# Feed-forward products of a hybrid attention block: the stationary operand read as every other number of 1 KB

## The chip, the cores and the metric

The kernel runs on one core of one Trainium2 chip. The metric is the device time of one execution in microseconds (us); the time of a kernel is the median of its runs. Matmuls run on TensorE (PE in the profile, its weight loads PEld), elementwise work on VectorE (DVE), ScalarE (ACT) and GpSimd (POOL); SyncE (SP) issues transfers.

## The reference, cut to what matters

One block of a network for 512 tokens of width 1024: attention over selected keys, a recurrent branch, gates, a first layer norm, a feed-forward part of width 4096, a gated addition and a second layer norm. The change concerns the feed-forward part:

```
D_MODEL = 1024
SEQ = 512
D_FF = 4 * D_MODEL
...
        h = layer_norm(DEEPNORM_ALPHA * h + merged @ w_out[l], ln1_g[l], ln1_b[l])
        ff = jnp.square(jax.nn.relu(h @ w_ff1[l])) @ w_ff2[l]
        r = DEEPNORM_ALPHA * h + ff
        r = r + jax.nn.sigmoid(r @ w_ple_gate[l]) * (p[l] @ w_ple_proj[l])
        h = layer_norm(r, ln2_g[l], ln2_b[l])
```

All inputs and outputs are float32.

## The kernel before, in words

Every large product is made from operands that are split in two numbers of the type float32r, a high part and a low rest, and three matmuls take the place of one: high by high, high by low, low by high. ACT makes the high part (a cast), DVE or POOL the rest (a subtraction).

The first feed-forward product, `h @ w_ff1`, lies in `ff1` (the matmul is at L969). Its columns are done in four groups of 1024. In each group the product is seen as one of matrices of 2 by 2 blocks and made with seven block products, `P1` to `P7`, in place of eight; sums of blocks go in, and `ff1_sums` puts the results together. So there are 28 steps. In a step the stationary operand is 128 columns of a block of the weights (`w1h`, `w1l`, made by `w1_factor`), four such pieces `b`; the moving operand is 256 tokens of a block of the transposed h (`hcH`, `hcL`, made by `h_factors` with `split` at L114 and L120). For each of the four pieces there are three kinds of product of four matmuls each over the 512 rows of the block: 48 matmuls a step, 1344 in all, and before each of them its stationary operand is loaded. A matmul writes 128 by 256 numbers.

The second product, `relu(...)^2 @ w_ff2`, lies in `ff2` (the matmul is at L1200), again as seven block products for each of four blocks of rows: 28 steps. Here the stationary operand is 128 tokens of the activations (`ah`, `al`), two such pieces `s`, and the moving operand 512 columns of the weights (`wh`, `wl`): 24 matmuls a step, 672 in all, each with a load of its own. A matmul writes 128 by 512 numbers.

`issue_after` chains the matmuls of both products in the order in which they are written; ACT's and DVE's work for them goes in the order of `queued`. The operands of a step are made while the step before it runs, in pairs of buffers. Weights come by transfers into `w1q` and `b`; some blocks get a second block added by a transfer that accumulates, which POOL issues (L896 and L1050). The two kinds of step take turns only at one place: the first of `ff2`'s steps is issued before the last of `ff1`'s.

In the built program every operand of both products begins 32 bytes past a multiple of 64 bytes. Counted in 256 bytes, the stationary operand that is loaded next begins 64 bytes after the place where the moving operand begins in `ff1`, and at the same place in most of `ff2`.

Of the kernel before, what the change touches and what calls it, by code (L numbers as in the profile page):

```python
# [7 lines left out]
F32 = mybir.dt.float32  # L8
# [6 lines left out]
P = 128  # L15
S = 512
D = 1024
# [6 lines left out]
DFF = 4096  # L24
# [30 lines left out]
    return ap.bitcast(F32)  # L55


@with_exitstack
def block_kernel(ctx: ExitStack, tc: tile.TileContext, t, out):
    nc = tc.nc  # L60
    te, ve, se, ge, sy = nc.tensor, nc.vector, nc.scalar, nc.gpsimd, nc.sync
# [8 lines left out]
    def open_pool(name, side=None, space=None, reuse="tile"):  # L70
        kw = {}
        if side:
            kw["side"] = side
        if space:
            kw["space"] = space
        cm = tc.tile_pool(name=name, bufs=1, reuse_waits=reuse, **kw)
        p = cm.__enter__()
        return p, (lambda: cm.__exit__(None, None, None))
# [9 lines left out]

    def misc(name):
        return ps_pool.tile([P, 512], F32, tag="misc", bufs=4, name=name)  # L90

    const, close_const = open_pool("const", side="left")
# [4 lines left out]
    rawpool, close_raw = open_pool("raw", side="right")  # L99
# [13 lines left out]
    def split(src, hi, lo, lo_eng=None, copy=None):  # L113
        (copy or se.copy)(hi, src)  # L114
        low(lo_eng or ve, lo, src, hi)

    def low(eng, lo, src, hi):

        if eng is not ge:
            return eng.tensor_sub(lo, src, f(hi))  # L120
        w = src.shape[-1]
        for j in range(src.shape[1]):
            for c in range(0, w, 256):
                o = slice(c, min(c + 256, w))
                eng.tensor_sub(lo[:, j][..., o], src[:, j][..., o], f(hi[:, j][..., o]))
# [30 lines left out]
    def transpose4(dst, src, k0):  # L156
        for k in range(4):
            t_ = te.transpose(dst[:, k * P:(k + 1) * P], src[:, (k0 + k) * P:(k0 + k + 1) * P], ident)
        return t_
# [6 lines left out]
    for _ in range(20):  # L166
# [7 lines left out]
    ge.affine_select(out=bias0, in_=bias0, compare_op=OP.is_ge, fill=MASKED, base=0,  # L174
                     pattern=[[-1, P]], channel_multiplier=1)
    mhalf = const.tile([P, 16], F32, name="mhalf")
    ve.memset(mhalf, -0.5)


# [47 lines left out]
    for k in range(KD):  # L227
        wh, wl = (w[:, k % 2] for w in kvw[k // 2][1:])
        for kind in range(3):
            for i in range(NT):  # L230
                te.matmul(b1[i][:, :208], (xH, xL, xH)[kind][:, k, i * P:(i + 1) * P], (wh, wh, wl)[kind],
                          start=k == 0 and kind == 0, stop=k == KD - 1 and kind == 2)
# [20 lines left out]
    def stacks(src, n, name, tag, bufs):  # L253

        st = att.tile([P, n, P], F32R, tag=tag, bufs=bufs, name=name)
        for g in range(n // 4):
            ps = misc(name + "p")
            transpose4(ps, src.rearrange("p n a b -> p (n a b)"), g * 4)
            v = ps.rearrange("p (h q) -> p h q", h=4)
            o = st[:, g * 4:g * 4 + 4, :]  # L260
            se.copy(o, v)
            ve.tensor_sub(o[64:128], v[64:128], f(o[64:128]))
        return st
# [58 lines left out]
    for i in range(NT):  # L322
        ve.tensor_scalar(wi[:, i, :], b1[i][:, 192:200], IDX_W, None, op0=OP.mult)
        ps = misc("kp")
        for n, o in enumerate((128, 0)):
            k2 = att.tile([P, 1, 2, 64], F32, tag="k2", bufs=2, name="k2")
            rope(b1[i][:, o:o + 64], i, 1, k2, ve)
            te.transpose(ps[:, n * P:(n + 1) * P], k2.rearrange("p n a b -> p (n a b)"), ident)
        split(ps[:, 0:P], kiH[:, i * P:(i + 1) * P], kiL[:, i * P:(i + 1) * P])
        split(ps[:, P:2 * P], kaH[:, i * P:(i + 1) * P], kaL[:, i * P:(i + 1) * P])  # L330
        split(b1[i][:, 64:128], vHL[:, i, 0:64], vHL[:, i, 64:128])
        se.copy(vH0[:, i, 0:64], b1[i][:, 64:128])
# [9 lines left out]
    for i in range(1, NT):  # L342
        n = (i + 1) * P
        q2 = q2s[i % 2]
        rope(b3[i], i, HEADS, q2, ve)
        st = stacks(q2, HEADS, "qi", "qs", 2)
        sc = att.tile([P, n], F32, name=f"sc{i}")
        for h in range(HEADS):
            ps = misc("lg")
            te.matmul(ps[:, :n], st[:, h, :], kiH[:, :n], start=True, stop=False)  # L350
            te.matmul(ps[:, :n], st[:, h, :], kiL[:, :n], start=False, stop=True)
            rl = att.tile([P, S], F32, tag="rl", bufs=2, name="rl")[:, :n]
            se.activation(rl, ps[:, :n], AF.Relu)
            if h == 0:
                ve.tensor_scalar(sc, rl, wi[:, i, h:h + 1], None, op0=OP.mult)
            else:
                ve.scalar_tensor_tensor(sc, rl, wi[:, i, h:h + 1], sc, op0=OP.mult, op1=OP.add)
        ge.affine_select(out=sc[:, i * P:], in_=sc[:, i * P:], compare_op=OP.is_ge, fill=NEG_CAUSAL, base=0,
                         pattern=[[-1, P]], channel_multiplier=1)
        scores[i] = sc  # L360
# [356 lines left out]
    hcH, hcL = {}, {}  # L717
# [57 lines left out]
    def h_factors(i):  # L775

        o = slice(i % 2 * P, i % 2 * P + P)

        def put(n, ps):
            split(ps.rearrange("p (k q) -> p k q", k=4), hcH[n][:, :, o], hcL[n][:, :, o])  # L780

        ps = [misc("hps0"), misc("hps1")]
        for kk in range(2):
            turned[:] = [transpose4(ps[kk], r[:, i, :], kk * 4)]
        if i < 2:
            for kk in range(2):
                se.copy(hb[kk][:, :, o], ps[kk].rearrange("p (k q) -> p k q", k=4))
                put((A11, A12)[kk], ps[kk])
            return
        a22 = ln.tile([P, 512], F32, tag="a22", bufs=1, name="a22")  # L790
        se.copy(a22, ps[1])
        put(A22, ps[1])
        v = [p_.rearrange("p (k q) -> p k q", k=4) for p_ in ps]
        ve.tensor_sub(ps[1], ps[0], a22)
        p2, p3 = misc("hps2"), misc("hps3")
        v2, v3 = (p_.rearrange("p (k q) -> p k q", k=4) for p_ in (p2, p3))
        ve.tensor_sub(v2, v[1], hb[0][:, :, o])
        ve.tensor_add(v3, v2, hb[1][:, :, o])
        put(S4, p3)
        put(S1, ps[1])  # L800
        ve.tensor_sub(v[0], hb[0][:, :, o], v[0])
        put(S3, ps[0])
        put(S2, p2)
# [146 lines left out]
    def w1_banks(t, n):  # L950
        e = t % 2 * 3
        return sets[{P1: e, P6: e, P2: 3 - e if t else 1, P5: 1}.get(n, 2)]
# [3 lines left out]
    def ff1(t, n, ws):  # L956

        hi, lo = ws
        ah, al = hcH[HALF[n]], hcL[HALF[n]]
        for kinds in (((hi, ah), (hi, al)), ((lo, ah),)):  # L960
            for b in range(4):
                ps = w1_banks(t, n)[b // 2][:, b % 2 * 256:b % 2 * 256 + 256]

                def product():
                    for w, a in kinds:
                        for k in range(4):

                            fresh = n not in (P6, P4) and w is hi and a is ah and k == 0 and b % 2 == 0
                            mm = te.matmul(ps, w[:, k, b * P:(b + 1) * P], a[:, k], start=fresh, stop=w is lo and k == 3,  # L969
                                           skip_group_check=True)  # L970
                    mms.append(mm)

                if mms:
                    with tc.issue_after(mms[-1].ins):
                        product()
                else:
                    product()
# [203 lines left out]
    banks, before = {}, []  # L1181
# [9 lines left out]
    def ff2(d, n, e, ops):  # L1191

        (wh, wl), (ah, al) = ops
        fresh = e == 0 and (d == 0 if n in (P1, P6) else n in (P5, P2, P4, P7))
        for s, kind in ((0, 0), (0, 1), (1, 0), (1, 1), (0, 2), (1, 2)):
            tok = slice(s * P, (s + 1) * P)

            def product():
                for q in range(4):
                    mm = te.matmul(banks[n, s], (al if kind == 1 else ah)[:, q, tok], (wl if kind == 2 else wh)[:, q],  # L1200
                                   start=fresh and kind == 0 and q == 0, stop=kind == 2 and q == 3, skip_group_check=True)
                before.append(mm)

            if before:
                with tc.issue_after(before[-1].ins):
                    product()
            else:
                product()
# [79 lines left out]
    for k, (d, n, e) in enumerate(steps):  # L1288
# [32 lines left out]
        if (d, n, e) in GATE_STEPS:  # L1321
            load_gate(0, GATE_STEPS.index((d, n, e)))
        ff2(d, n, e, ops)
        if (d, n) == (1, P4):
            gate_inputs(e)
# [82 lines left out]
```

## Time and profile before

| | |
|---|---|
| runs | 770.44, 774.37 and 776.04 us, median 774.37 us |
| the profiled execution | 776.13 us, of which 774.4 us from the first instruction to the last |
| PE busy in it | 760.9 us (98%), 4332 matmuls and 4332 loads |
| the other engines | DVE 596.9 us (77%), ACT 419.4 us (54%), POOL 268.7 us (35%) |
| matmuls of `ff1` (L969) | 407.5 us to 569.6 us |
| matmuls of `ff2` (L1200) | 560.1 us to 720 us |

A matmul is shown longer than the distance to the next one, because matmuls are pipelined: how fast they go is read from the distance between two starts, or from the time that a row of many took together, and not from the mean of one. The chain of work that ended last is followed back from the last instruction; 20% of the span on it is L969 and 20% L1200.

### The profile page before, as it was taken

The page shows a single profiled execution, that of the slowest core. Times are in us where ns is not written, and L with a number is a line of the kernel's source. Part 1 is how long each engine was busy: PE and PEld are TensorE (multiplying, and loading weights), DVE is VectorE, ACT ScalarE, POOL GpSimd, SP SyncE. Part 2 cuts the span into 40 slices and gives each one's busy share as a digit, 9 for nine tenths or more (in the row PEclk, how much of TensorE's full clock was granted, in tenths as well). Part 3 has the DMA queues.
Part 4 walks back from the last instruction along what each step waited for, and adds up shares of the span by engine and source line. Part 5 has one row for each costly group of instructions (what it writes and reads, how often), then busy time and mean ns, then how long its engine had stood idle before and what let it go on. Part 6 is the DMA issues. An engine that isn't in the chain of part 4 may idle for free.

```text
span 774.4 us, 11502 instructions
## 1 busy us (share of the span) xinstructions
PE 760.9 (98%) x4332; PEld 664.3 (86%) x4332; DVE 596.9 (77%) x988; ACT 419.4 (54%) x637; POOL 268.7 (35%) x332
## 2 busy tenths in 40 slices
PE   9899999999999999999999999999999999999995
PEld 8678888888988888878889999999988888888885
DVE  6669999966547987477796757576788988998558
ACT  5346556698756543443266575656565555656221
POOL 7627464434346445670142120303010101116341
PEclk9999999999999999999999999999999999999999
DMA  7424232232232202348069996947597799895302
GB/s 236 136 55 129 64 81 56 82 96 56 55 83 81 69 15 68 96 142 327 22 213 196 330 255 191 236 103 113 112 222 195 135 390 315 145 185 181 102 27 109
DMA packets 78072, 110.43 MB, mean 143 GB/s; under 512 B 3776, under 2 KB 39104, under 8 KB 76736
## 3 DMA queue, kind: packets, MB, share of 16 engines
q1 hardware_dynamic: 59664, 72.78, 28.5%
q0 software_dynamic: 13920, 27.27, 20.5%
q10 hardware_dynamic: 4432, 9.65, 3.6%
q8 instruction: 34, 0.56, 0.3%
q14 instruction: 22, 0.18, 0.1%
HBM read 101.29 MB, written 8.39 MB: 142 GB/s over the span
## 4 chain that ended last, share of the span: by engine, by line
PE 87%; DVE 7%; POOL 2%; DMA 2%; issue 1%; ACT 1%; SPq 0%; DVEq 0%; POOLq 0%; ACTq 0%
PE pf L969 20%; PE pf L1200 20%; PE pg L152 4%; PE pg L154 4%; PE pg L153 4%; PE po L152 2%; PE po L153 2%; PE po L154 2%; PE pu L152 1%; PE pu L154 1%; PE pu L153 1%; PE ptp L460 1%; POOL wul L145 1%; PE mqc L152 1%; PE mo L152 1%; PE mv L153 1%
## 5 line engine op out<-in xcount | busy, mean ns | idle before, releaser
L823 DVE TENSOR_TENSOR w1l<-w1q,w1h 128x1024 fp32r<-128x1024 f32 x55 | 64.9, 1222 | 35.6 <-ACT w1h L823 35.0
L823 DVE TENSOR_TENSOR wl<-b,wh 128x2048 fp32r<-128x2048 f32 x28 | 64.7, 2312 | 10.7 <-ACT wh L823 10.7
L823 ACT CAST w1h<-w1q 128x1024 fp32r<-128x1024 f32 x55 | 55.2, 1048 | 24.4 <-PE pf L969 19.8
L896 POOL DMA_DIRECT2D w1q<-in_w_ff x24 | 29.2, 1254 | 111.9 <-DVE w1l L823 108.0
L145 POOL TENSOR_TENSOR wgl<-wgr,wgh 128x256 fp32r<-128x256 f32 x64 | 50.3, 819 | 44.8 <-ACT wgh L142 40.4
L1050 POOL DMA_DIRECT2D b<-in_w_ff x14 | 17.9, 1279 | 133.2 <-DVE wl L823 133.2
L1200 PE MATMUL pf<-wh,ah 128*128 128x512 f32 x216 | 58.1, 391 | 0.0
L1200 PE MATMUL pf<-wh,al 128*128 128x512 f32 x216 | 57.8, 389 | 0.0
L823 ACT CAST wh<-b 128x2048 fp32r<-128x2048 f32 x28 | 53.5, 1909 | 3.5 <-DMA b<-in_w_ff 3.5
L1200 PE MATMUL pf<-wl,ah 128*128 128x512 f32 x216 | 53.5, 390 | 0.0
L154 PE MATMUL pg<-xH,wgl 128*128 128x512 f32 x128 | 50.5, 395 | 0.0
L153 PE MATMUL pg<-xL,wgh 128*128 128x512 f32 x128 | 50.3, 393 | 0.0
L152 PE MATMUL pg<-xH,wgh 128*128 128x512 f32 x128 | 50.1, 391 | 0.0
L1200 PEld LDWEIGHTS pf<-wh,al 128*128 128x128 f32 x216 | 40.6, 188 | 8.5
L1200 PEld LDWEIGHTS pf<-wh,ah 128*128 128x128 f32 x216 | 40.3, 188 | 8.7 <-ACT wh L823 0.4
L1200 PEld LDWEIGHTS pf<-wl,ah 128*128 128x128 f32 x216 | 40.5, 188 | 8.4
L145 POOL TENSOR_TENSOR wul<-wur,wuh 128x128 fp32r<-128x128 f32 x64 | 35.3, 584 | 21.5 <-ACT wuh L142 17.7
L823 DVE TENSOR_TENSOR c<-c,pf 128x512 f32<-128x512 f32 x48 | 30.5, 682 | 10.2 <-ACT c L823 10.2
L823 ACT ACTIVATE c<-c 128x1024 f32<-128x1024 f32 x12 | 12.7, 1060 | 31.3 <-DVE c L823 31.3
L744 POOL TENSOR_TENSOR lag<-lag,mhalf 128x1 f32<-128x1 f32 x8 | 7.6, 950 | 62.9 <-DVE lag L743 62.9
L153 PEld LDWEIGHTS pg<-xL,wgh 128*128 128x128 f32 x128 | 24.0, 188 | 4.5
L152 PEld LDWEIGHTS pg<-xH,wgh 128*128 128x128 f32 x128 | 24.1, 188 | 4.5
(396 smaller groups left out, 2309.1 us busy)
## 6 DMA issues: line engine op xcount, KB each, us to landing
b<-in_w_ff POOLq DMA_DIRECT2D x14, 1024.0 KB, 9.0
w1q<-in_w_ff POOLq DMA_DIRECT2D x24, 512.0 KB, 7.5
w1q<-in_w_ff SPq DMA_DIRECT2D x9, 1024.0 KB, 5.7
wgr<-in_w_in SPq DMA_DIRECT2D x16, 512.0 KB, 3.8
b<-in_w_ff SPq DMA_DIRECT2D x8, 1024.0 KB, 8.2
wor<-in_w_out SPq DMA_DIRECT2D x8, 512.0 KB, 3.9
b<-in_w_ff ACTq DMA_DIRECT2D x4, 1024.0 KB, 6.0
wpgr<-in_w_ple_gate SPq DMA_DIRECT2D x8, 512.0 KB, 8.9
```

The costliest lines, as they stand in the source:

```text
L145: (lo_eng or ge).tensor_sub(lo[:, k:k + n], raw[:, k:k + n], f(hi[:, k:k + n]))
L152: te.matmul(ps, sh, mh, start=first, stop=False, **kw)
L153: te.matmul(ps, sh, ml, start=False, stop=False, **kw)
L154: return te.matmul(ps, sl, mh, start=False, stop=last, **kw)
L460: te.transpose(ps[:, slot * P:(slot + 1) * P], prs[slot // 2][:, slot % 2, j * P:(j + 1) * P], ident)
L744: ge.tensor_tensor(out=ag[:, 3:4], in0=ag[:, 2:3], in1=mhalf[:, 0:1], op=OP.pow))
L823: order_of[engine] = getattr(engine, op)(*args, **kw)
L896: ge.dma_start(out=tl[:, k], in_=w1_rows(t, W1_ADD[n])[:, k], accum_op=OP.add)
L969: mm = te.matmul(ps, w[:, k, b * P:(b + 1) * P], a[:, k], start=fresh, stop=w is lo and k == 3, skip_group_check=True)
L1050: return ge.dma_start(out=tl, in_=rows_of(g, w), accum_op=OP.add)
L1200: mm = te.matmul(banks[n, s], (al if kind == 1 else ah)[:, q, tok], (wl if kind == 2 else wh)[:, q], start=fresh and kind == 0 and q == 0, ...
```

## The change

A helper `alternate` gives every other number of a row: of 256 numbers (1 KB) the even ones are the block 0, the odd ones the block 1. The stationary operands of both products are read so: 128 numbers, 8 bytes apart, over 1 KB, where they were 128 numbers in a row, over 512 bytes.

For `ff1` the columns of `w_ff1` are put in that order in the input's memory ahead of the launch, so that the pieces `b` 0 and 1, and 2 and 3, alternate. For `ff2` the tokens alternate: `h_factors` writes the 128 tokens of a block to every other place of `hcH` and `hcL`, so the activations come out in the same order, and `ff2` reads its pieces `s` 0 and 1 from even and odd places. The moving operands are read in a row as before, and the results of `ff2` have the tokens of one block in a row again.

Two unused tiles, of 32 and of 224 bytes, move what lies behind them in the two halves of the on-chip memory: in the built program all operands of the two products begin at multiples of 64 bytes (the odd block 4 bytes further), and the distance in 256 bytes between stationary and moving operand is what it was. DVE fills the two tiles once at the start. Besides these two fills every engine has the same instructions in the same order.

```
+def alternate(ap, which):
+
+    return ap.rearrange("p k (j s) -> p k s j", s=2)[:, :, which]
...
     mhalf = const.tile([P, 16], F32, name="mhalf")
+    ve.memset(const.tile([P, 8], F32, name="pad"), 0.0)
+    ve.memset(rawpool.tile([P, 56], F32, name="rawpad"), 0.0)
     ve.memset(mhalf, -0.5)
...
         def put(n, ps):
-            split(ps.rearrange("p (k q) -> p k q", k=4), hcH[n][:, :, o], hcL[n][:, :, o])
+            split(ps.rearrange("p (k q) -> p k q", k=4), alternate(hcH[n], i % 2), alternate(hcL[n], i % 2))
...
-                            mm = te.matmul(ps, w[:, k, b * P:(b + 1) * P], a[:, k], start=fresh, stop=w is lo and k == 3,
+                            mm = te.matmul(ps, alternate(w[:, :, b // 2 * 256:b // 2 * 256 + 256], b % 2)[:, k], a[:, k], start=fresh, stop=w is lo and k == 3,
                                            skip_group_check=True)
...
         for s, kind in ((0, 0), (0, 1), (1, 0), (1, 1), (0, 2), (1, 2)):
-            tok = slice(s * P, (s + 1) * P)
+            at = alternate(al if kind == 1 else ah, s)
...
-                    mm = te.matmul(banks[n, s], (al if kind == 1 else ah)[:, q, tok], (wl if kind == 2 else wh)[:, q],
+                    mm = te.matmul(banks[n, s], at[:, q], (wl if kind == 2 else wh)[:, q],
                                    start=fresh and kind == 0 and q == 0, stop=kind == 2 and q == 3, skip_group_check=True)
...
+    arrays["in_w_ff1"] = np.ascontiguousarray(arrays["in_w_ff1"].reshape(1, D, DFF // 256, 2, P)
+                                              .transpose(0, 1, 2, 4, 3).reshape(1, D, DFF))
```

## Rows read from the trace of the kernel before

**Rows 1.** The page: busy time of each engine.

```profile
PE 760.9 (98%) x4332; PEld 664.3 (86%) x4332; DVE 596.9 (77%) x988; ACT 419.4 (54%) x637; POOL 268.7 (35%) x332
```

**Rows 2.** The chain that ended last: start us, us, what (the feed-forward part).

```profile
407.63 152.64 PE pf L969 x1296
...
563.99 5.66 PE pf L969 x48
569.65 138.18 PE pf L1200 x608
```

**Rows 3.** Busy time by stretch: stretch, its us, engines, clock, DMA share, GB/s.

```profile
407.40:560.00 152.60, 152.60 (x1297) 152.56 (x1297) 106.77 (x116) 93.21 (x111) 27.82 (x23) 1.00 0.80 193
...
569.60:720.00 150.40, 150.40 (x670) 124.12 (x669) 134.87 (x106) 82.53 (x63) 33.17 (x29) 1.00 0.86 223
```

**Rows 4.** Timeline of PE: another product with moving operands of 256 columns.

```profile
182.39 0.28 PE L152 MATMUL mv<-mvwh,xH 128*128 128x256 f32 x1
...
184.98 0.28 PE L153 MATMUL mv<-mvwl,xH 128*128 128x256 f32 x1
...
185.65 0.28 PE L152 MATMUL mv<-mvwh,xH 128*128 128x256 f32 x1
...
186.67 0.28 PE L152 MATMUL mv<-mvwh,xH 128*128 128x256 f32 x1
```

**Rows 5.** Timeline of PE: two rows of matmuls with moving operands of 512 columns.

```profile
59.70 0.40 PE L153 MATMUL aq<-aqwl,xH 128*128 128x512 f32 x1
...
60.86 0.39 PE L152 MATMUL aq<-aqwh,xH 128*128 128x512 f32 x1
...
97.81 0.39 PE L154 MATMUL pg<-xH,wgl 128*128 128x512 f32 x1
...
99.17 0.39 PE L154 MATMUL pg<-xH,wgl 128*128 128x512 f32 x1
```

**Rows 6.** The chain: eight transposes, moving operands of 128 columns.

```profile
380.78 0.87 PE hps L158 x8
```

**Rows 7.** Timeline of PE and its stretch at half the clock: 512 columns.

```profile
28.87 0.63 PE L154 MATMUL iq<-iqwh,xL 128*128 128x512 f32 x1
...
30.15 0.63 PE L154 MATMUL iq<-iqwh,xL 128*128 128x512 f32 x1
...
27.40:30.70 3.30, 3.30 (x10) 2.51 (x9) 1.99 (x11) 3.05 (x10) 1.86 (x2) 0.50 0.01 2
```

**Rows 8.** Who waited for whom, 560 to 725 us: us in total, times, longest.

```profile
ACT ah L823 <- PE pf L1200: 53.8, 23, 2.6
...
ACT wh L823 <- DMA b<-in_w_ff: 3.5, 2, 2.3
...
PEld pf L1200 <- ACT wh L823: 0.4, 1, 0.4
```

**Rows 9.** Who waited for whom, 400 to 560 us.

```profile
ACT w1h L823 <- PE pf L969: 19.8, 10, 2.7
```

**Rows 10.** Groups by form, 375 to 425 us: the writes of `hcH` and `hcL`, one each.

```profile
L114 ACT CAST hc0H<-hps 128x512 fp32r<-128x512 f32 x2 | 1.2, 599 | 0.0
L120 DVE TENSOR_TENSOR hc0L<-hps,hc0H 128x512 fp32r<-128x512 f32 x2 | 1.4, 677 | 1.4 <-ACT hc0H L114 1.4
```

**Rows 11.** Timeline of DVE and PE at the start.

```profile
1.16 0.07 DVE L177 MEMSET mhalf<- 128x16 f32 x1
...
1.26 4.63 PE L167 MATMUL idle<-warm 128*128 128x256 f32 x20 [1.26 <-DVE mhalf L177]
```

## The prediction

> **What bounds the kernel now.** I read the page first: PE is busy for 98% of the span, no other engine for more than 77% [rows 1]. Then the chain of waits: through the feed-forward part it is PE alone, matmul after matmul, with no wait of another engine in between [rows 2]. [...] So whatever one matmul of these two products gains or loses goes to the end of the span, 1344 and 672 times, as long as ACT, DVE and the transfers keep up.
>
> How far apart do the matmuls stand? In the first product 1296 of them take 152.64 us, 117.8 ns each, and the last 48 take 5.66 us, 117.9 ns each; in the second 608 take 138.18 us, 227.3 ns each [rows 2]. How much of that could go is read from other products of the same shapes in this trace. With 256 moving columns the distance has two values, each held for a whole row of matmuls: from 182.39 to 184.98 us there are 22 distances, 117.7 ns each, and from 185.65 to 186.67 us nine, 113.3 ns each, in the same product with the same kind of operands [rows 4]. With 512 columns the usual value is (99.17 - 97.81)/6 = 226.7 ns; the five distances from 59.70 us have 232 ns [rows 5]. And 113.3 is half of 226.7: this looks like the pace of the moving operand alone, with 4.4 ns of something else on top in most products of 256 columns.
>
> What the something is, rows only hint at. The load by itself is short enough: transposes with 128 moving columns, where the load is the longer part, stand 0.87/8 = 109 ns apart [rows 6], below 113. Load and moving operand read the same memory at the same time, and their relative place is fixed by the addresses and the start of the row; that two levels hold over whole rows of equal instructions [rows 4] speaks for readers that do or don't get in each other's way. The first product sits at the upper level throughout.
>
> **The change part by part.** *The load of the first product.* In the time of one matmul the moving operand goes through 1 KB. The load went through 512 bytes and now goes through 1 KB: the two readers go at the same pace, a fixed distance apart, where before one passed over the other. If the 4.4 ns come from their meeting, a fixed distance of 64 bytes takes them away: 1344 x (117.8 - 113.3) = -6.0 us. This is the value that I take, since the lower level is the nearest row with the same shape, and no row of 256 columns at full clock goes below it. The bounds are far on both sides: 109 ns (the load alone, [rows 6]) would be -11.8 us; 4.4 ns twice over 113.3 ns, because the load now touches twice as much memory, would be 122.2 ns, +5.9 us.
>
> [...]
>
> *The load of the second product.* It has 227 ns to hide in, and the distance is within 0.6 ns of the lower level already: 672 x (227.3 - 226.7) = -0.4 us if all of it goes. I take -0.3 us. [...] On the other side the 232 ns of rows 5 would be +3.2 us.
>
> *Other operands at multiples of 64 bytes.* The some 1400 matmuls of 512 columns outside the feed-forward part keep their shapes and steps; most are at the lower level of rows 5. I take 0; bounds -1.2 us and +1.2 us (a sixth of them changes between the 232 and the 226.7 ns of rows 5).
>
> *The writes of `hcH` and `hcL` at every other place.* There are 14 casts on ACT of about 0.6 us and 14 subtractions on DVE of about 0.68 us [rows 10], same sizes as before. I take their length as unchanged. If each took half as long again, ACT would have 4.2 us and DVE 4.8 us more, spread from 381 to 414 us; PE has the projections of the second input to do meanwhile, and at the end of this stretch only a microsecond or two of it could show, +1 us at most.
>
> *The two fills on DVE.* They stand ahead of the fill `mhalf`, for whose end the twenty warm-up matmuls wait [rows 11]. Two of about 0.07 us delay these by 0.15 us; the first real matmuls wait for their inputs afterwards, so I count 0.1 us.
>
> *What is late next.* If PE gets faster by 4% in the first product, its step of 48 matmuls shrinks from 5.65 to 5.44 us. ACT waits for PE there 10 times, 19.8 us in all [rows 9], and DVE is busy 107 of 152.6 us [rows 3]: both follow. In the second product DVE is busy 134.87 of 150.4 us [rows 3], 90%, and ACT waited for PE 23 times [rows 8]; one load of weights came just too late, 0.4 us of PE [rows 8]. With a second product as it was, this stays.
>
> The sum: -6.0 - 0.3 + 0.1 = -6.2 us. The profiled execution took 776.13 us, its span 774.4 us; the difference is set up around it and stays. The median of the runs, 774.37 us, lies 1.8 us below the profiled execution, so I take the sum from the median: 768.2 us.
>
> **The rivals.**
>
> *More is freed than the lower level.* If the moving operand's own pace of 226.7 ns were also the work of loads, both products could fall to what rows 6 and 7 bound: the first to 109 ns (-11.8 us), the second to 213 ns (-9.4 us), in all 753 us; DVE would then have 134.87 us of work in 141 us and would begin to delay steps, so 755 us is nearer. [...]
>
> *The change doesn't do what it says.* The 4.4 ns may have nothing to do with where the load reads: the first product stays at 117.8 ns, 774 us. For: rows 4 switch levels with the same operands in the same order, so the start of a row matters, not only addresses. [...]
>
> *The two readers meet more often.* A load that touches 1 KB has twice the chances to get in the way of the moving operand, and where they go at the same pace at the same place, as in the second product, they may do so all along. Then the first product goes to 122.2 ns (+5.9 us) and the second to the 232 ns of rows 5 (+3.2 us): 783.5 us. It decides from the point where the first product's distance is above 118 ns. For: the 232 ns of rows 5 show that with 512 columns, too, a matmul can be held up. Worse still, a load of twice the length, 218 ns, would set the distance of the first product: 1344 x 100 ns, +134 us, 908 us. Nothing in the trace excludes it, since none of its loads has a step.
>
> **How the numbers follow.** The forecast, 766 to 770 us, has 0.4; more freed (752 to 762 us) 0.17; no effect (773 to 776 us) 0.2; more meetings (778 to 788 us) 0.2; the long load 0.03. The range 754 to 784 us leaves out half of the first and third rival's ends and the long load. A measurement of this kernel tells about 1%, 7.7 us, from no change. Faster by over that, below 766.6 us: the first rival and the lower part of the forecast, where the other products gain too, 0.3. Slower by over 1%, above 782.1 us: most of the third rival and the long load, 0.2. The rest, 0.5, is within 1%.
>
> **What would show it.** In the changed kernel's chain the 1296 matmuls of the first product should take 147 us in place of 152.64, and 608 of the second 137.8 us. [...] The loads shown should stay as long as they are. The prediction is wrong above all if loads with a step take longer than loads in a row, which this trace can't show, or if the levels are set by the start of a row and not by the addresses.

## The result, and the profile after

| | runs | median | lowest to highest |
|---|---|---|---|
| before | 4 | 772.64 us | 770.44 to 776.04 us |
| after | 4 | 784.14 us | 783.21 to 784.93 us |

The ratio on record is 1.0133, with a 95% interval of 1.0093 to 1.0172 (the two medians by themselves give 1.0149): the change makes the kernel slower by 10 to 11.5 us, where 6 us less had been forecast. Every run of after lies above every run of before. The profiled execution of after took 784.38 us, its span 782.7 us, against 776.13 and 774.4 us before: 8.3 us more.

The page first, busy time of each engine in the kernel after:

```profile
PE 768.2 (98%) x4332; PEld 671.0 (86%) x4332; DVE 597.9 (76%) x990; ACT 420.0 (54%) x637; POOL 267.8 (34%) x332
```

The same 4332 matmuls have 7.3 us more of PE, and PE is still busy for 98% of the span. DVE has two instructions more, the fills, and 1 us more work. So the lost time is to be looked for in the distances of matmuls. The chain of the kernel after (start us, us, what), to be laid beside [rows 2]:

```profile
407.93 155.52 PE pf L977 x1296
563.45 3.69 PE pf L1208 x16
567.14 5.76 PE pf L977 x48
572.90 24.26 PE pf L1208 x104
...
665.27 50.66 PE pf L1208 x216
```

In the first product 1296 matmuls take 155.52 us, 120.0 ns each, where they took 117.8 ns; the last 48 take 5.76 us, 120.0 ns as well. In the second, 104 take 24.26 us, 233.3 ns each, where it was 227.3 ns. Those 227.3 ns hold the 0.4 us that PE lost behind a late load of weights [rows 8]; without it they are (138.18 - 0.4)/608 = 226.6 ns, the usual value of [rows 5]. The starts of the pieces add up to the whole: the first product begins 0.3 us later than in [rows 2], the second 3.25 us later, and its 608 matmuls end at 665.27 + 50.66 = 715.93 us, 8.1 us later than before (569.65 + 138.18 = 707.83). So the first product has cost 2.95 us and the second 715.93 - 572.90 - 138.18 = 4.85 us.

Was PE held up by others? The stretches of the two products in after (stretch, its us, then busy us and instructions of PE, PEld, DVE, ACT and POOL, granted clock, DMA share, GB/s):

```profile
407.70:563.30 155.60, 155.60 (x1298) 155.56 (x1298) 107.22 (x117) 93.81 (x112) 27.82 (x23) 1.00 0.79 190
572.90:728.00 155.10, 154.17 (x667) 127.36 (x667) 135.08 (x106) 82.00 (x63) 33.37 (x29) 1.00 0.85 217
```

Granted clock and work of the other engines are nearly those of [rows 3]. PE has no idle time in the first stretch and 155.10 - 154.17 = 0.93 us in the second. That is one late load. Timeline of ACT and of PE in after at that place (in brackets the idle time before, and who ended it):

```profile
663.31 1.91 ACT L831 CAST wh<-b 128x2048 fp32r<-128x2048 f32 x1 [3.44 <-DMA b<-in_w_ff]
```
```profile
665.27 1.20 PE L1208 MATMUL pf<-wh,ah 128*128 128x512 f32 x4 [0.93 <-ACT wh L831]
```

A transfer into `b` landed late, ACT's cast of it waited 3.44 us, and PE lost 0.93 us behind the cast. So of the 8.1 us, 0.3 lie ahead of the feed-forward part, 2.95 in the first product and 608 x (233.3 - 226.7) = 4.0 in the distances of the second; the 0.8 us left are what late loads cost more in this execution than in that of before.

The loads themselves, a group of the second product from 570 to 720 us, in after:

```profile
L1208 PEld LDWEIGHTS pf<-wh,ah 128*128 128x128 f32 x208 | 40.0, 193 | 9.6 <-ACT wh L831 1.4
```

The mean load is shown with 193 ns, and 64 loads of the first product with 194 ns in the middle. In the kernel before both groups have 188 ns. Both grew by 5 to 6 ns.

### The profile page after: what moved, and what is told of

It reads as the page before. It is cut to its first block, busy times and chain, and to the rows that moved or that the text cites. A ratio compares the mean times of both kernels' runs of the same rounds, so it can differ in the third digit from the quotient of the medians.

```text
span 782.7 us, 11504 instructions
## 1 busy us (share of the span) xinstructions
PE 768.2 (98%) x4332; PEld 671.0 (86%) x4332; DVE 597.9 (76%) x990; ACT 420.0 (54%) x637; POOL 267.8 (34%) x332
## 4 chain that ended last, share of the span: by engine, by line
PE 80%; DVE 10%; DMA 5%; issue 4%; ACT 1%; SPq 0%; POOL 0%; DVEq 0%; POOLq 0%; ACTq 0%
PE pf L977 21%; PE pf L1208 11%; PE pg L158 4%; PE pg L160 4%; PE pg L159 4%; DMA b<-in_w_ff 3%; PE pu L160 2%; PE po L160 2%; PE po L159 2%; PE po L158 2%; PE pu L158 2%; PE pu L159 2%; PE ptp L468 1%; PE mqc L158 1%; PE mo L158 1%
## 5 line engine op out<-in xcount | busy, mean ns | idle before, releaser
L831 ACT CAST ah<-uH 128x1024 fp32r<-128x1024 f32 x12 | 12.6, 1052 | 29.2 <-PE pf L1208 29.2
```

The source lines that it names most:

```text
L831: order_of[engine] = getattr(engine, op)(*args, **kw)
```

## The experiments

The theory after this result: **the step makes the load longer**, and in the first product the load (120.0 ns) now outlasts the moving operand (113.3 ns) and sets the distance. The rivals: the new beginnings of the operands do it, not the step; or the step makes load and moving operand get in each other's way, as the third rival of the prediction says. One question came with it: where do the 4.4 ns between 113.3 and 117.8 ns come from, if no step takes them away?

**The step alone** (`e1_step_alone`): the two tiles go, so the operands begin 32 bytes past a multiple of 64 bytes, as before.

```
-    ve.memset(const.tile([P, 8], F32, name="pad"), 0.0)
-    ve.memset(rawpool.tile([P, 56], F32, name="rawpad"), 0.0)
```

> The step of two numbers alone, without the two unused tiles: all operands again 32 bytes past a multiple of 64. Theory A (the step costs, the alignment does nothing): first product 120.0 ns a matmul, second 233.3 ns, as with the whole change, 782 us. Theory B (the alignment costs, the step is harmless or good): first product at 117.8 ns or 113.3 ns, second at 226.7 ns, 768 to 774 us.

Measured: 782.87 us median of 4 runs (782.65 to 783.31), 1.0148 times the kernel before (1.0093 to 1.0203). The chain of this kernel:

```profile
408.00 155.52 PE pf L975 x1296
572.97 141.84 PE pf L1206 x608
```

The same 120.0 and 233.3 ns, as theory A has it, and no late load this time. Its span, 781.6 us, is 7.2 us above that of before: 155.52 - 152.64 = 2.9 us in the first product and 141.84 - 138.18 = 3.7 us in the second make up 6.6 of it. So the loss belongs to the step, and beginnings at multiples of 64 bytes are not needed for it.

**Steps of 1, 2, 4 and 1 in the four groups** of the first product (`e2_steps_by_group`), the rest as after:

```
+STEP = (1, 2, 4, 1)
...
+    def piece(t, w, b):
+        s = STEP[t]
+        o = b // s * s * P
+        return alternate(w[:, :, o:o + s * P], b % s, s)
...
+                            mm = te.matmul(ps, piece(t, w, b)[:, k], a[:, k], start=fresh, stop=w is lo and k == 3,
```

> All operands at multiples of 64. The four groups of the first product read their stationary operand with steps of 1, 2, 4 and 1 numbers (the input's columns are put in the order that fits); the second product as in the change. Theory A1 (what counts is how much memory the load goes through: 512 bytes, 1 KB, 2 KB): 117.8, 120.0, about 124 to 127, 117.8 ns. [...] Theory A3 (load and moving operand meet when they go at the same pace; at another pace they don't stay together): step 4 no worse than 118 to 120 ns. Theory B (alignment): the groups with step 1 are at 120 ns too.

Measured: 818.22 us, one run. The chain of this kernel, one piece from each group:

```profile
408.95 35.13 PE pf L985 x310
...
446.97 38.04 PE pf L985 x317
...
486.91 77.26 PE pf L985 x328
...
566.96 30.15 PE pf L985 x266
```

113.3, 120.0, 235.5 and again 113.3 ns. The distance goes with the step, group by group in one execution. A1's 124 to 127 ns and A3's 118 to 120 ns don't fit the 235.5 ns at a step of 4. Why a step of 2 costs 6.7 ns was not shown. And the groups in a row stand at 113.3 ns here, without any step: the lower level that the prediction wanted is there when nothing but the tiles has changed, or by chance. That is taken up below.

**The same with half the moving operand** (`e3_steps_half`). Each matmul of the first product takes 128 of its 256 tokens; half of the product is left out. Then the load should be the longer of the two at every step (109 ns in a row, from [rows 6], against half of 113.3 ns for the moving operand, an estimate), and the distance shows it by itself: if the step makes the load longer, 120.0 ns stay at a step of 2; if the two get in each other's way, steps of 1 and 2 are alike.

```
-                            mm = te.matmul(ps, piece(t, w, b)[:, k], a[:, k], start=...
+                            mm = te.matmul(ps[:, k % 2 * P:k % 2 * P + P], piece(t, w, b)[:, k],
+                                           a[:, k, k % 2 * P:k % 2 * P + P], start=...
```

> As the kernel with the steps by group, but each matmul of the first product takes only 128 of its 256 tokens (even k the first half, odd k the second), so half of the first product's work is left out and the load is the longer part: the distance is the load's own time. [...] Theory A3 (two readers in each other's way, the load by itself as long as ever): 109 ns with step 1 and 2 alike, or nearly.

Measured: 846.73 us. Pieces of this kernel's chain with steps of 1, 2 and 4:

```profile
409.00 35.06 PE pf L985 x314
...
445.91 38.16 PE pf L985 x318
...
485.86 76.36 PE pf L985 x327
```

111.7, 120.0 and 233.5 ns. With half of the moving operand the distances at steps 2 and 4 are what they were with all of it. So 120.0 ns is the load's own length, and not a meeting with the moving operand, which has only half the time to meet in. (A load in a row, 111.7 ns, is a little longer than the 109 ns that the prediction read from transposes.) The third stretch must be read with care, since the clock fell in it (columns as above):

```profile
446.00:484.00 38.00, 38.00 (x319) 38.00 (x319) 26.61 (x29) 21.97 (x27) 7.25 (x6) 1.00 0.86 228
485.50:488.30 2.80, 2.80 (x14) 2.80 (x13) 1.87 (x2) 1.84 (x2) 0.28 (x1) 1.00 1.12 202
488.50:562.00 73.50, 73.50 (x316) 73.50 (x317) 26.44 (x29) 25.39 (x29) 6.77 (x6) 0.50 0.38 87
```

The comparison of steps 1 and 2 lies at a granted clock of 1.00. That of step 4 lies at 0.50, but for its beginning. Timeline of PE there:

```profile
485.22 1.10 PE L985 MATMUL pf<-hc0H,w1h 128*128 128x128 f32 x4
...
488.03 0.91 PE L985 MATMUL pf<-hc0L,w1h 128*128 128x128 f32 x3
```

Twelve distances in 2.81 us at a granted clock of 1.00 are 234 ns each, so step 4 takes the same at both levels, and nearly the 235.5 ns of the run above.

**Four distances, with the step** (`e4_distance_scan`). In the first product the stationary operand begins 192, 0, 64 and 128 bytes, counted in 256 bytes, after the moving operand, one distance for each group; in the second 128 bytes.

```
+        hi, lo = (pools[1].tile([P, 2112], F32R, tag="w1" + x, ...)[:, 16 * t:16 * t + 2048]
+                  .rearrange("p (a b) -> p a b", a=4) for x in "hl")
...
+                gap.append(late.tile([P, 32], F32, name="gap"))
```

> Steps of 2 and multiples of 64 as in the change, but the stationary operand begins 192, 0, 64 and 128 bytes (in 256) after the moving one in the four groups of the first product, and 128 in place of 0 bytes in the second. [...] Theory A3 (at the same pace the distance decides whether they meet): distances differ by 4 ns or more, some at 113.3 ns; the second product moves away from 233.3 ns, towards 226.7 ns.

Measured: 783.41 us. A piece each from the first, second and fourth group, and one of the second product:

```profile
408.93 38.08 PE pf L978 x313
...
448.95 39.12 PE pf L978 x326
...
529.95 33.06 PE pf L978 x273
...
573.59 24.08 PE pf L1214 x104
```

121.7, 120.0 and 121.1 ns (the third group has 120.0 ns too); 231.5 ns in the second product. No distance goes below 120 ns, so the prediction's "fixed distance" has nothing to work on: the load comes first. The place of the two operands adds 1.7 ns at most in the first product, and 128 bytes take 1.8 ns off the 233.3 ns of the second.

**The two tiles alone** (`e5_tiles_alone`), with loads in a row: before, and the two fills.

> The two unused tiles alone: all operands at multiples of 64 bytes, every load again 128 numbers in a row. Theory D (the alignment takes 4.4 ns from the first product, the step costs more than that in both): first product 113.4 ns, second 226.7 ns, 6 us less than before, 764 to 768 us. Rival (the two groups at 113.4 ns in the run with steps by group owe it to what lies beside them): 117.8 ns and no difference.

Measured: 769.89 us median of 12 runs against 775.12 us of 17, ratio 0.9945 (0.9919 to 0.9971). Its chain:

```profile
408.52 146.88 PE pf L971 x1296
564.57 137.88 PE pf L1202 x608
```

113.3 ns: the whole forecast gain of the first product, without the step. It looked as if beginnings at multiples of 64 bytes were the cause. Two scans asked whether beginning or distance counts: loads in a row, distances of 64, 96, 128 and 192 bytes in the four groups, the moving operand at a multiple of 64 bytes (`e6_row_scan_at_64`) or 32 bytes past one (`e7_row_scan_at_32`).

```
+        hi, lo = (pools[1].tile([P, 2112], F32R, ...)[:, (0, 8, 16, 32)[t]:(0, 8, 16, 32)[t] + 2048]
```

> As the kernel with the two tiles alone, but in the four groups of the first product the stationary operand begins 64, 96, 128 and 192 bytes (in 256) after the moving one: in the second group it is 32 bytes past a multiple of 64 while the moving operand is at one. Theory D1 (the load's own alignment counts): 113.4, 117.8, 113.4, 113.4 ns. Theory D2 (the moving operand's alignment counts): 113.4 ns in all. Theory D3 (the distance counts): differences between 64, 128 and 192.

> The kernel before, but with the same four distances: the moving operand 32 bytes past a multiple of 64 throughout, the stationary one at a multiple of 64 in the second group alone. Theory D1 (the load's own alignment): 117.8, 113.4, 117.8, 117.8 ns. Theory D2 (the moving operand's): 117.8 ns in all. Theory D3 (the distance): differences between 64, 128 and 192 bytes.

Measured: 775.87 and 774.08 us. Two pieces of the first one's chain:

```profile
408.93 36.15 PE pf L972 x319
...
446.94 38.64 PE pf L972 x322
```

From such pieces of all groups, in ns:

| distance | 64 | 96 | 128 | 192 bytes |
|---|---|---|---|---|
| at a multiple of 64 | 113.3 | 120.0 | 118.7 | 117.8 |
| 32 past one | 117.8 | 117.3 | 118.7 | 117.8 |

So a matmul with a load in a row can be held up too, by an amount that changes with the distance inside one unbroken row of matmuls, up to the 120.0 ns of a load with a step. Beginnings alone don't explain it: at 64 the first line of the table falls to 113.3 and at 192 it doesn't. Each line is one execution, so what it shares with the level of that execution can't be told apart: at 64 bytes the two lines show just the two levels.

**Is it the beginning, or the execution?** The kernel of the two tiles was run again in 12 runs (`e13_tiles_again`), and beside it one in which two small unrelated tiles, `invf` and `wi`, are moved to another pool, while beginnings and distances stay (`e14_tiles_and_moved`).

```
-    invf = const.tile([P, 32], F32, name="invf")
+    invf = att.tile([P, 32], F32, name="invf")
...
-    wi = const.tile([P, NT, HEADS], F32, name="wi")
+    wi = att.tile([P, NT, HEADS], F32, name="wi")
```

> The two unused tiles alone, a second time and with more executions: are loads in a row at multiples of 64 bytes what puts the first product on the lower of its two levels (113.3 and 117.8 ns, 6 us apart in all)? Theory H (the alignment does it): most executions near 769 us, as in the first run of this kernel, while the kernel before is spread over both levels. Theory I (the moment at which a row of matmuls starts decides, whatever the alignment): about the same share of both levels in both kernels.

> The two unused tiles, and two small tiles of the attention part in another pool, so that everything in the left half lies 256 bytes lower: the same alignment and the same distances in both products as with the two tiles alone; this is the first product of the four runs with two kinds of loads in the second, three of which stood at 117.8 ns and one at 113.3 ns. Theory H (alignment): most executions near 769 us. Theory I (the start of the row): both levels, a good part of them near 775 us.

Measured: 771.95 us median against 773.64 us of 23 runs of before, ratio 1.0004 (0.997 to 1.0038); and 770.0 us, ratio 0.9989 (0.9955 to 1.0023). The chain of the first, the same program as the one with 146.88 us above:

```profile
407.82 152.64 PE pf L971 x1296
```

117.8 ns. So one program stood at 113.3 ns in one execution (770.69 us) and at 117.8 ns in another (776.60 us): the addresses alone don't set the level. The difference of 5.9 us is that of the row, 1344 x 4.43 ns = 6.0 us. `e14_tiles_and_moved` stood at 113.3 ns (146.88 us for 1296, 771.22 us in all). The runs fit: of before's 23 runs beside it 11 lie between 768.26 and 770.57 us and 12 between 773.64 and 777.53 us, and none between. The gain measured in `e5_tiles_alone` was one of shares: 11 of its 12 runs were in the lower cluster and 14 of the 17 beside it in the upper; in the second series it was 6 of 12, against 11 of 23. Such shares move from series to series for one program, so an interval that takes the runs for independent is too narrow. Whether the tiles shift the share stays open: all series together have 17 of 24 runs of the two tiles, 8 of 12 with the tiles moved, and 21 of 52 of before in the lower cluster.

**The second product.** There the load (120 ns) lies well within the 227 ns of the moving operand, and still the step costs 6 ns. Is it the length of the load? `e8_shorter_loads` gives one kind of matmul 128 numbers with the step, one 64 with the step and one 64 in a row; half of the two small corrections of the product is left out.

```
+                    if kind == 0:
+                        st, bank = at[:, q], banks[n, s]
+                    else:
+                        st = at[:, q, 0:64] if kind == 1 else ah[:, q, s * P:s * P + 64]
+                        bank = banks[n, s][0:64]
```

> The changed kernel; in the second product the matmuls with the activations' low part load only 64 numbers (step 2), those with the weights' low part 64 numbers in a row, so half of the two small corrections is left out (and the last is taken for other tokens); high by high loads 128 numbers with step 2 as in the change. Theory E (each piece of memory that a load touches takes time from the moving operand): 233.3 ns for 128 numbers with step 2, about 230 ns for 64 with step 2, 226.7 ns or a little less for 64 in a row. Rival (the moving operand is slower for another reason than the load's length, such as the order of the tokens): 233.3 ns for all three.

Measured: 779.69 us; 608 matmuls in 140.31 us, 230.8 ns each. By kind: 230.3, 231.5 and 229.2 ns. Half the load with the step isn't faster than the whole one, and the load in a row is not at 226.7 either. Neither theory fits; the run is inconclusive.

Is it the distance? Four kernels, one for each distance in the second product (`e9_second_at_0`, `e10_second_at_64`, `e11_second_at_128`, `e12_second_at_192`), have half of its blocks with the step and half in a row, and the first product in a row. The blocks in a row take other tokens than the reference's, so that part of the sum is another.

```
+            a = al if kind == 1 else ah
+            at = a[:, :, s * P:(s + 1) * P] if e else alternate(a, s)
...
+                gap.append(late.tile([P, 48], F32, name="gap"))
```

> First product in a row, all at multiples of 64. In the second product the blocks of rows take turns: every other one loads its activations with step 2, the others in a row (so those take other tokens: the output is another one, the work the same). Distance 0 as in the change. Theory F (step 2 costs the second product 6.7 ns, whatever the first product does): 233.3 ns with step 2, 226.7 ns in a row, first product 113.3 ns. Rival (its 6.7 ns came from the state in which the first product left the queue): 226.7 ns for both.

> The same with the stationary operand of the second product beginning 64 bytes (in 256) after the moving one. Theory G1 (the step costs there at every distance): step 2 at 231 to 235 ns. Theory G2 (there is a distance at which the readers stay clear of each other at the same pace): 226.7 ns at one of 64, 128 and 192 bytes. In a row: 231 to 236 ns, as some rows of 512 columns of the kernel before have.

> The same at 128 bytes. Theory G1: step 2 at 232 ns, as in the scan of distances; in a row 226.7 to 231 ns. Theory G2: 226.7 ns with step 2 at one of the three distances.

> The same at 192 bytes. Theory G1: step 2 at 231 to 235 ns; in a row 226.7 to 236 ns. Theory G2: 226.7 ns with step 2 at one of the three distances.

Measured: 777.74, 778.49, 778.7 and 773.82 us. The distances in ns, from steps of the second product without idle time:

| distance | 0 | 64 | 128 | 192 bytes |
|---|---|---|---|---|
| step of 2 | 233.3 | 233.3 | 231.3 to 231.6 | 233.2 |
| in a row | 226.8 | 233.2 | 232.1 to 232.8 | 229.0 |

The chain of `e10_second_at_64`, both kinds together, 233.2 ns each:

```profile
568.30 141.78 PE pf L1214 x608
```

Against 226.7 ns, a load in a row is free only where it begins at the moving operand's place, as it did before; at the other three it costs 2 to 6.5 ns. A load with a step costs 4.6 to 6.6 ns at all four, as theories F and G1 have it, and no distance was found at which it is free. So the step costs something only at 0 and at 192 bytes: at 64 both kinds take the same, and at 128 the load in a row is the slower one. One execution for each distance shows this.

That an execution has its level here too is seen in the second product of `e2_steps_by_group`, the same as in the kernel after, with the step at distance 0:

```profile
609.94 88.20 PE pf L1216 x378
...
699.84 35.33 PE pf L1216 x150
```

233.3 ns before and 235.5 ns behind a delay of some 60 ns at 698.7 us.

The chain of `e9_second_at_0` shows one thing more, pieces of the first product in one execution:

```profile
407.07 152.64 PE pf L977 x1296
...
563.39 5.46 PE pf L977 x48
```

117.8 ns in the long row, and 113.8 ns in the last 48, after 16 matmuls of the second product. Same line, same operands' beginnings, same execution: the level changed where the row was entered anew. It need not: in the kernel before the last 48 stay at 117.9 ns [rows 2]. And of these four runs the first three have 117.8 ns in the long row and `e12_second_at_192` 113.3 ns, though its operands begin at the same places in all four.

## Why the prediction was wrong

**The step that failed is "The load of the first product"**: a fixed distance of 64 bytes was to take 4.4 ns away and leave 113.3 ns, -6.0 us. The first product went to 120.0 ns, +3.0 us against the profiled execution of before. Two premises were wrong. The load was held to stay below 113 ns, from transposes whose loads were in a row [rows 6]; with the step it takes 120.0 ns by itself, as the run with half the moving operand shows. That a step leaves the load as long as it is was the author's assumption; no row of before has a load with a step. And the 4.4 ns were taken as something that a choice of addresses removes; the repeated kernel shows both levels with the same addresses, so the forecast 113.3 ns could have come, or failed to come, without any change. The prediction had named just these two as what would make it wrong, and had seen the second in [rows 4], where the same product switches levels; it should have weighed more.

In the run with half the moving operand a step of 4 doubles the load (111.7 to 234 ns), and a step of 2 adds 8.3 ns (111.7 to 120.0 ns). Why a load with a step is longer was not shown; the 8.3 ns are what puts the load past the moving operand (113.3 ns).

**"The load of the second product"**, -0.3 us, was +4.0 us: 233.3 ns in place of 226.7. The 0.6 ns above the lower level, from which the -0.3 us were taken, were the 0.4 us of the late load, the same that "What is late next" leaves standing; there was nothing to gain. The bound given there on the slow side, 232 ns and +3.2 us, was nearly it. That the load "has 227 ns to hide in" was no protection, though it is only 120 ns long. Where the two operands begin counts as well: the table by distance has 226.8 and 233.2 ns for loads in a row at 0 and 64 bytes, one execution each.

**Other terms.** The casts that write `hcH` take 610 to 664 ns, where they took 582 to 626 ns, and the subtractions 676 to 690 ns, as before. So "unchanged" was short by some 35 ns a cast, but nothing of that reached the end: the 0.3 us by which the first product begins later are there already at the first of the transposes that these casts read, 381.12 us against 380.78 us [rows 6]. Among all runs with a first product in a row its beginning differs by more, 405.3 to 409.1 us. The fills cost nothing that shows either: the warm-up begins at 1.26 us in both kernels [rows 11], and in after it waits for another fill, which stands ahead of the two. The lines of after:

```profile
381.12 0.87 PE hps L164 x8
```
```profile
1.26 4.63 PE L173 MATMUL idle<-warm 128*128 128x256 f32 x20 [1.26 <-DVE warm L170]
```

The late load that "stays" went from 0.4 us [rows 8] to 0.93 us of PE in this execution; in the run with the step alone there was none, so it comes and goes with a transfer and is no part of the change.

**The rivals.** "The two readers meet more often" gave 783.5 us, and 784.14 us was measured. Its condition came true (above 118 ns), but that the times lie so close is in part luck: it had 5.9 us for the first product, which lost 3.0, and 3.2 us for the second, which lost 4.0, and the rest is a late load and a median of before that was still at 774.37 us. Its cause isn't needed for the first product, where the load alone explains 120.0 ns, and is neither shown nor refuted for the second. A load of twice the length is what a step of 4 has (234 against 111.7 ns), not of 2 (120.0 ns). That more is freed has no support: with whole loads no step of the two products went below 113.3 ns with 256 or 226.7 ns with 512 columns at full clock. The 213 ns that this rival adds up are an estimate, half of the 427 ns that [rows 7] have at a granted clock of 0.50; no run shows them at 1.00. What held is the reading of the bound: PE without idle time, everything else keeping up, and every nanosecond of distance passed on to the end.

**From 8.3 to 11.5 us.** The medians differ by more than the two profiled executions, because before's was one with the upper level, 117.8 ns, while half of its four runs, 770.44 and 770.91 us, lie with those that had 113.3 ns when profiled. Against these the first product loses 1344 x 6.7 = 9.0 us. The four runs of after and the four with the step alone (782.65 to 784.93 us) show no such clusters: at 120.0 ns the load is longer than either level, which fits.

**Still open**: why a load with a step of 2 is 8.3 ns longer, why it holds up a moving operand of nearly twice its length, which is half of what the change cost, and what picks the level of a row. A version that beats both kernels was not found; the two tiles alone were 0.5% faster in one series and the same as before in the next, and the moved tiles were the same.

## What to carry to other kernels

A stationary operand read with a step was not free here (120.0 against 111.7 ns a load at a step of 2): compare the load's own length (measured with a short moving operand) with the moving operand's, and don't lengthen the load where it would come near it (120.0 against 113.3 ns in the first product). Even where the load was half as long as the moving operand, the step cost 6.6 ns a matmul here. Where equal instructions stand at two levels inside the trace of one kernel, don't forecast a gain from moving addresses before the same program was seen in several executions; profile it more than once, and look whether its runs fall in clusters. For loads in a row, a stationary operand that begins at the same place in 256 bytes as the moving one cost nothing in the second product, and other distances up to 6.5 ns a matmul, in one run each.

## What the runs showed of the hardware

- A load of 128 float32r numbers takes 111.7 ns in a row, 120.0 ns with a step of 2 and 234 ns with a step of 4 at a granted clock of 1.00, read from matmuls of 128 moving columns in `e3_steps_half`. At a granted clock of 0.50 in the same run, 314 matmuls with a step of 4 took 73.28 us, 233 ns each, and 165 in a row 35.20 us, 213 ns each: the load in a row takes nearly twice as long at half the clock, the one with a step of 4 the same.
- In that run, with 128 moving columns, PE worked without idle time, matmul after matmul of 128 columns, from 409 us on at a granted clock of 1.00; from 488.5 us it was granted 0.50.
- Rows of matmuls with 256 moving columns and loads in a row stood at two levels, 113.3 and 117.8 ns, in different executions of one program and, after another row in between, in one execution; in this kernel the choice is worth 6 us. Of the 88 runs of the kernel before and of the two with the tiles and without the step, none lies between 771.3 and 773.4 us.
- In the second product the distance of matmuls with loads in a row was 226.8, 233.2, 232.1 to 232.8 and 229.0 ns where the stationary operand began 0, 64, 128 and 192 bytes (in 256) after the moving one.
